# A Mamba-2 layer in fp32 halves: x's forms at other steps, the third form from a second load of x, and another order of pieces, filler and drains at two blocks of the output

## The chip, the cores and the metric

One core of one Trainium2 chip runs the whole layer. The metric is the device time of one execution in microseconds (us). TensorE (PE) multiplies, with its weight loads counted apart (PEld); VectorE (DVE) and ScalarE (ACT) work element by element; GpSimd (POOL) is used here for little but issuing the DMAs that add to what stands in SBUF; SyncE (SP) issues nearly all other DMAs, in order, and stands at one whose buffer isn't free yet.

## The reference

One layer (DEPTH is 1, so the pooling mixer isn't reached) of a Mamba-2 mixer on a sequence of 512 tokens, with an RMSNorm before it, a residual around it and a final RMSNorm. D_MODEL is 2048, D_INNER 4096, with 64 heads of 64, 8 groups, a state of 128.

```python
hn = rmsnorm(x, ln_g[0])
proj = hn @ w_in                     # 2048 -> 4096 z + 6144 (x, B, C) + 64 dt
z, xbc, dt = split(proj)
xbc = silu(causal_depthwise_conv(xbc, conv_w, conv_b))    # 4 taps
xs, B, C = split(xbc)
dt = softplus(dt + dt_bias)
a = -exp(a_log)
y = ssd_chunked_scan(xs * dt, dt * a, B, C)               # chunked state-space scan
y = (y + d_skip * xs) * silu(z)
y = rmsnorm(y, norm_g)
return rmsnorm(x + y @ w_out, final_g)
```

## The kernel before, in words

All large products are made in fp32 accuracy from halves: a tensor is split into `hi` (rounded to fp32r by a ScalarE cast, line 88) and `lo` (the rest, a VectorE subtraction, line 89), and a product is three matmuls, hi·hi, hi·lo and lo·hi. The transposed x, scaled by the norm's weight, lies in SBUF as `xh` and `xl`, 16 tiles of 128 x 512.

**Plain products.** The first eight projections, `plain`, are made directly: B0 and C0 together while x and the first weights come in, then x0, z0, x1, z1, B1 and C1, each of 16 steps (one step is the six matmuls of `mm_k`, line 211). Steps are numbered through the program: x0 begins at 32, z0 at 48, x1 at 64, z1 at 80, B1 at 96, C1 at 112, and step 128 ends them. The weights come in pieces of 8 steps (512 KB). `get_piece` loads one raw into one of the rings `ra` (3 buffers), `rb` (1) or `rc` (2) and splits it. A piece is named by its number; pieces 10 and 11 belong to z1 (steps 80 to 95), 15 to C1's second half (from step 120).

**Strassen quads.** The other 72 projections go in 36 pairs (`pair`). Each is a 2 x 2 product of blocks done with seven products instead of eight, 28 steps (`QS`) in all. For that the weights are summed into the forms T1, T2, T3 and T4 (T1 and T3 by a POOL DMA that adds in SBUF, T2 and T4 by a VectorE addition, line 618), and x into forms 1, 2, 4 (`x_forms`) and 3 (`x_form3`). `x_forms(g, j)` makes a quarter of the forms 1, 2 and 4: SP loads two halves of x once more, into `csb` and `m` (j = 0) or `h1h` and `h1l` (j = 1), ScalarE scales them, then come three VectorE combinations in an `rc` buffer (lines 576, 577, 579) and three splits (ScalarE line 573, VectorE line 574): six VectorE operations of 128 x 512 a call. `x_form3(j)` makes one of four quarters of the third form in place of the second half of `xh` and `xl`: four VectorE operations (lines 588, 589, 590, 592) through the one buffer `xr`, and a ScalarE copy. The seventh product of a quad (`last`) runs as filler between the second and the third of the next; for the first quad there is no such filler, and it begins with T1 and then R11 (`lone`).

**What runs beside it.** The dt path: 16 products, softplus on VectorE (`dt_softplus`, lines 353 to 364), cumulative sums, totals and spread (`dt_cumul`, `dt_sums`, `dt_spread`), all through the one PSUM tile `tr`; its result `sn` is stored to `cscr`, from where each unit's `csb` is loaded back for its decay (`u_load`, `u_decay`). Then for each of 32 units the convolution, transposes (line 486, into `tr`), the scan's products, the gate and a store of y.

**The output.** `blocks` gives the order: plain blocks are lists of (column quarter s, pairs of y tiles), each (s, pair) a piece of 8 steps (`mm_o`, lines 948 to 950); tuples are Strassen blocks of four `opair`s of seven products (`oproduct`, lines 886 to 888), whose forms of y are made by `y_fetch` (loads) and `y_forms`. Pieces of several pairs in one tuple of `blocks` are summed in one PSUM group, and a line of VectorE (1065) adds the group to `acc`; the accumulations of a Strassen block are lines 908, 921, 926 and so on. `load_y(p)` loads and splits the y of pair p (split on VectorE at line 758). The last plain block before a Strassen block may leave two of its four row tiles over as filler (`bridge`), which then run as `prev` between the second and third product; before, that is done at block 2 alone, and the first Strassen block runs without filler.

**What sets the order.** `add(step, f, ...)` puts an event at a step and `run(step)` issues it there. PE, SP and POOL run in the order in which the program is written; VectorE and ScalarE are ordered by the Tile scheduler, where `urgent` gives priority.

Of the kernel before, what the change touches and what calls it, by code (L numbers as in the profile page):

```python
# [18 lines left out]
P = 128  # L19
# [16 lines left out]
def mamba_layer(ctx: ExitStack, tc: tile.TileContext, d: dict, out: bass.AP):  # L36
# [99 lines left out]
    def every(*pairs):  # L136
        return [(s, pairs) for s in range(4)]

    blocks = [[(0, (0,))] + every(0, 1)[1:] + [(0, (1, 2))] + every(2)[1:], (2, 3), every(3, 12), (4, 5),
              every(13), every(14, 15)]  # L140
# [7 lines left out]
    for i, blk in enumerate(blocks):  # L148
        late = 4 if i == 0 or i > 2 and type(blocks[i - 1]) is tuple else 0
        base.append(base[-1] + (4 * QS if type(blk) is tuple else 8 * n_pieces(blk) + late))  # L150
# [404 lines left out]
    def x_forms(g, j):  # L555
# [4 lines left out]
        for n, k0 in ((n1, k), (n2, KH + k)):  # L560
            nc.sync.dma_start(n, d["xT"][:, k0:k0 + 2, :])
            for i in range(2):
                S.activation(n[:, i, :], n[:, i, :], AF.Identity, scale=lng[:, k0 + i:k0 + i + 1])
        if j == 0:
            for f, s in ((1, 0), (2, 4), (4, 8)):
                form[f, g] = [xp.tile(SSH, F32R, name=f"s{s + 2 * g + i}") for i in range(2)]
# [14 lines left out]
        put(4, t1)  # L581

    def x_form3(j):

        kk = slice(2 * j, 2 * j + 2)
        h, lo = xh[:, kk, hi_], xl[:, kk, hi_]
        t = xr[:, 3:L + 3].rearrange("p (k l) -> p k l", k=2)
        V.tensor_tensor(out=t, in0=xh[:, kk, lo_], in1=h, op=ALU.subtract)
        V.tensor_tensor(out=t, in0=t, in1=xl[:, kk, lo_], op=ALU.add)
        V.tensor_tensor(out=t, in0=t, in1=lo, op=ALU.subtract)  # L590
        S.copy(out=h, in_=t)
        V.tensor_tensor(out=lo, in0=t, in1=h, op=ALU.subtract)  # L592

# [132 lines left out]
    for g in range(1, G):  # L726
        for i in range(2):
            add(at["x", 4 * g] + 34, g_cb, g, i)
        add(at["x", 4 * g] + 34, g_bt, g)
    steps = {0: [66, 71, 63, 104, 104, 114], 1: [56, 76, 72, 108, 108, 114], NU - 1: [36, 46, 44, 65, 65, 71]}  # L730
    for u in range(5, NU - 4, UPG):
# [7 lines left out]
    for i in range(4):  # L739
        add(49 + 7 * i, x_forms, i // 2, i % 2)  # L740
        add(114 + 4 * i, x_form3, i)

# [40 lines left out]
    st = {}  # L783

    def norm_a():
        with urgent():
            st["rest"] = x_norm()
# [12 lines left out]
    add(b0 + 44, g_bt, 0)  # L800
    add(b0 + 26, dt_softplus)
    add(b0 + 37, g_cb, 0, 0)
# [179 lines left out]
    for i, blk in enumerate(blocks):  # L982
        if type(blk) is tuple:
            for s in range(4):
                q_events(len(quads) + 4 * m + s, base[i] + s * QS, s == 3, 0, 3 if s == 0 and not m else 0, s == 0 and not m)
            for j in range(2):
                add(base[i] - ((50, 32), (54, 32))[m][j], y_fetch, m, j)
                add(base[i] - ((39, 24), (47, 24))[m][j], y_forms, m, j)
            m += 1
# [39 lines left out]
    for kb, blk in enumerate(blocks[:-1]):  # L1029
# [10 lines left out]
        for s, pairs in blk:  # L1040
            ps = [None] * NC
            for p in pairs:
# [4 lines left out]
                for t in range(NC):  # L1047
                    if p == pairs[0]:
                        ps[t] = first.pop(0) if first else (ps_o or (ps_s, ps_mm)[t % 2]).tile(
                            [P, L], F32, name="mm" if ps_o or t % 2 else "S")  # L1050
                    if kb == 2 and n0 + 1 == n_end and t > 1:
                        bridge.append(partial(tail, ps[t], opieces[n0], ys[p], t, s))
                        continue
# [17 lines left out]
                n0 += 1  # L1071
                if n0 == 7:
                    ph1.close()
                    ps_o = ctx.enter_context(psum("ps_o", 6))
                    fp = ctx.enter_context(tc.tile_pool(name="fp", bufs=1))
                    load_y(2)
                    fg = fp.tile([P, DM], F32, name="fg")
                    nc.sync.dma_start(fg, d["fg"].partition_broadcast(P))
        if bridge:
            def prev(step, parts=bridge):  # L1080
                for i, f in enumerate(parts):
                    f(step + 2 * i)
                spare = ps_o.tile([P, L], F32, name="mm")
                T.transpose(spare[:, 0:P], ident, ident)

# [68 lines left out]
```

## Time and profile before

| | before |
|---|---|
| median of 3 runs | 1269.15 us (1267.62 to 1270.22) |
| the profiled execution | 1271.58 us, span 1269.6 us |
| granted TensorE clock, mean of the span | 0.992 |
| PE busy | 1235.1 us, 97% of the span |
| DVE busy | 1079.0 us, 85% |
| ACT busy | 829.0 us, 65% |
| POOL busy | 77.6 us, 6% |
| read from HBM | 211.52 MB |

The profile was taken of one execution; times in its rows are from the start of its span. A row of a timeline has its start, its duration, engine, line, operation, output and inputs, and in brackets the idle time of the engine ahead of it and what ended that. A row of waits has who waited for whom, then the total, how often and the longest. A row of windows has the stretch, its length, the busy time and the instructions of PE, PEld, DVE, ACT and POOL, then the granted clock (1 is full speed), the share of the DMA engines and GB/s. A row of DMA issues has the size of one and the median time from issue to landing.

### The profile page before, as it was taken

The numbers are of one execution on the slowest core, as the hardware profiler recorded it, in microseconds if no ns is written. First come the engines' busy times: TensorE is split into PE (matmuls) and PEld (weight loads), VectorE is DVE, ScalarE is ACT, GpSimd is POOL, SyncE is SP. The second block draws the span as 40 slices with busy tenths as digits, with TensorE's granted clock in tenths as the row PEclk, the third lists the DMA queues.
The fourth block names the chain that finished last, engine by engine and source line by source line (L and its number), as shares of the span: only waits on it lengthen the run. The fifth ranks groups of instructions, "written<-read, shape, count | busy, mean of one in ns | idle before, by whom it ended". The sixth has DMA issues, their size and how long they took to land.

```text
span 1269.6 us, 24517 instructions
## 1 busy us (share of the span) xinstructions
PE 1235.1 (97%) x9945; PEld 1178.0 (93%) x9945; DVE 1079.0 (85%) x1443; ACT 829.0 (65%) x1359; POOL 77.6 (6%) x99
## 2 busy tenths in 40 slices
PE   8989899999999999999999999999999899999997
PEld 7989899999999999999999999999888899899986
DVE  5796989998999998899989899988857887887865
ACT  7666677767767767876686777678666445444533
POOL 0000000010000000000001000000000000000000
PEclk9989999999999999999999999999999999999998
DMA  9546656767676667667676766775537576657612
GB/s 357 181 150 180 169 157 174 189 173 193 166 194 182 156 193 189 169 162 197 178 203 151 210 163 176 184 184 153 157 114 253 155 197 202 208 127 229 183 60 100
DMA packets 70193, 225.89 MB, mean 178 GB/s; under 512 B 8384, under 2 KB 12800, under 8 KB 69952
## 3 DMA queue, kind: packets, MB, share of 16 engines
q1 hardware_dynamic: 56688, 176.34, 39.5%
q0 software_dynamic: 12672, 46.14, 23.0%
q8 instruction: 78, 1.28, 0.4%
q10 hardware_dynamic: 720, 1.84, 0.4%
q14 instruction: 35, 0.29, 0.1%
HBM read 211.52 MB, written 12.78 MB: 177 GB/s over the span
## 4 chain that ended last, share of the span: by engine, by line
PE 61%; DVE 19%; ACT 8%; DMA 6%; issue 5%; SPq 0%; DVEq 0%; ACTq 0%
PE S L649 5%; PE S L651 5%; PE S L650 5%; DVE lo L89 4%; PE R L649 4%; PE R L650 3%; PE R L651 3%; PE mm L651 3%; PE mm L649 3%; PE mm L650 3%; PE mm L948 3%; PE mm L950 3%; PE mm L949 3%; PE mm L886 3%; PE mm L887 2%
## 5 line engine op out<-in xcount | busy, mean ns | idle before, releaser
L89 DVE TENSOR_TENSOR lo<-ra,hi 128x1024 fp32r<-128x1024 f32 x150 | 182.8, 1219 | 48.2 <-ACT hi L88 48.0
L88 ACT CAST hi<-ra 128x1024 fp32r<-128x1024 f32 x150 | 156.7, 1046 | 89.9 <-PE mm L887 23.5
L88 ACT CAST hi<-rc 128x1024 fp32r<-128x1024 f32 x94 | 98.9, 1053 | 99.0 <-PE mm L650 37.9
L649 PE MATMUL R<-s,hi 128*128 128x256 f32 x576 | 162.5, 282 | 0.0
L651 PE MATMUL mm<-xh,lo 128*128 128x256 f32 x576 | 159.2, 276 | 0.2 <-DVE lo L89 0.2
L649 PE MATMUL mm<-xh,hi 128*128 128x256 f32 x576 | 159.2, 276 | 0.2 <-ACT mm L705 0.2
L650 PE MATMUL R<-s,hi 128*128 128x256 f32 x576 | 159.2, 276 | 0.0
L651 PE MATMUL R<-s,lo 128*128 128x256 f32 x576 | 159.1, 276 | 0.0
L650 PE MATMUL mm<-xl,hi 128*128 128x256 f32 x576 | 159.1, 276 | 0.0
L89 DVE TENSOR_TENSOR lo<-rc,hi 128x1024 fp32r<-128x1024 f32 x94 | 114.3, 1216 | 3.9 <-ACT hi L88 3.7
L649 PEld LDWEIGHTS mm<-xh,hi 128*128 128x128 f32 x576 | 108.2, 188 | 0.6 <-ACT mm L705 0.6
L651 PEld LDWEIGHTS mm<-xh,lo 128*128 128x128 f32 x576 | 108.1, 188 | 0.4 <-DVE lo L89 0.4
L650 PEld LDWEIGHTS R<-s,hi 128*128 128x128 f32 x576 | 108.3, 188 | 0.0
L649 PEld LDWEIGHTS R<-s,hi 128*128 128x128 f32 x576 | 108.3, 188 | 0.0
L651 PEld LDWEIGHTS R<-s,lo 128*128 128x128 f32 x576 | 108.1, 188 | 0.0
L650 PEld LDWEIGHTS mm<-xl,hi 128*128 128x128 f32 x576 | 108.1, 188 | 0.0
L618 DVE TENSOR_TENSOR ra<-ra,rc 128x1024 f32<-128x1024 f32 x88 | 107.0, 1216 | 0.2
L651 PE MATMUL S<-xh,lo 128*128 128x256 f32 x288 | 79.7, 277 | 2.2 <-DVE lo L89 2.2
L649 PE MATMUL S<-xh,h1h 128*128 128x256 f32 x288 | 80.3, 279 | 1.0 <-ACT mm L705 1.0
L650 PE MATMUL S<-xl,hi 128*128 128x256 f32 x288 | 79.7, 277 | 0.7 <-DVE xl L592 0.7
L650 PE MATMUL S<-xl,h1h 128*128 128x256 f32 x288 | 80.3, 279 | 0.0
L651 PE MATMUL S<-xh,h1l 128*128 128x256 f32 x288 | 80.3, 279 | 0.0
(452 smaller groups left out, 3936.0 us busy)
## 6 DMA issues: line engine op xcount, KB each, us to landing
rc<-in_wi SPq DMA_DIRECT2D x76, 512.0 KB, 5.2
ra<-in_wi SPq DMA_DIRECT2D x42, 512.0 KB, 6.0
rb<-in_wi SPq DMA_DIRECT2D x40, 512.0 KB, 4.6
ra<-in_wi POOLq DMA_DIRECT2D x36, 512.0 KB, 6.2
rb<-in_wi POOLq DMA_DIRECT2D x36, 512.0 KB, 6.2
csb<-cscr SPq DMA_DIRECT2D x32, 512.0 KB, 5.6
ra<-in_wo SPq DMA_DIRECT2D x26, 512.0 KB, 5.2
yscr<-z SPq DMA_DIRECT2D x32, 256.0 KB, 4.4
```

The lines of the kernel that those rows point to most:

```text
L88: S.copy(out=hi, in_=raw)
L89: V.tensor_tensor(out=lo, in0=raw, in1=hi, op=ALU.subtract)
L618: V.tensor_tensor(out=raw, in0=raw, in1=qs[n][other], op=ALU.add)
L649: T.matmul(ps, hi[:, k, :], ah, start=first and k == 0, stop=False, skip_group_check=True)
L650: T.matmul(ps, hi[:, k, :], al, start=False, stop=False, skip_group_check=True)
L651: T.matmul(ps, lo[:, k, :], ah, start=False, stop=k == KH - 1, skip_group_check=True)
L886: T.matmul(ps[:, t, :], yh[:, k, tt], hi[:, k, :], start=st, stop=False, skip_group_check=True)
L887: T.matmul(ps[:, t, :], yl[:, k, tt], hi[:, k, :], start=False, stop=False, skip_group_check=True)
L948: T.matmul(ps, yh, hi, start=first and k == 0, stop=False)
L949: T.matmul(ps, yh, lo, start=False, stop=False)
L950: T.matmul(ps, yl, hi, start=False, stop=last and k == 1)
```

## The change

Three things are altered.

1. **Plain part.** `x_forms` runs at steps 38, 45, 66 and 92, in the order (1,1), (0,1), (0,0), (1,0), where it ran at 49, 56, 63 and 70 in the order (0,0), (0,1), (1,0), (1,1). Softplus is issued as urgent. The decay of unit 1 is 16 steps later.
2. **Third form.** A new `x_diff` loads a piece of x into an `ra` buffer at steps 106, 109, 122 and 124 and subtracts its second half of the tokens from its first in place. `x_form3`, now at 115, 118, 136 and 140 (before at 114, 118, 122 and 126), makes from that the high half by a scaling ScalarE activation and the low half by one VectorE operation, for each of its two tiles of 256 columns.
3. **Output.** The first plain block has another order of pieces: three pairs for s = 3 in one group, the first piece of s = 0 closed at the end. `y_fetch` and `y_forms` of the first Strassen block are 4 to 8 steps earlier with respect to its begin, the block gets the last piece's two tiles as filler and the order of the later blocks (no `lone`). The PSUM pool of the output, and `load_y(2)` with it, open after piece 6 and not 7. At both bridges a drain of TensorE stands where a spare transpose stood at the one.

```diff
-    blocks = [[(0, (0,))] + every(0, 1)[1:] + [(0, (1, 2))] + every(2)[1:], (2, 3), every(3, 12), (4, 5),
+    blocks = [[(0, (0,)), (1, (0, 1)), (2, (0, 1)), (3, (0, 1, 2)), (1, (2,)), (2, (2,)), (0, (1, 2))], (2, 3), every(3, 12), (4, 5),
...
-        late = 4 if i == 0 or i > 2 and type(blocks[i - 1]) is tuple else 0
+        late = 4 if i > 2 and type(blocks[i - 1]) is tuple else 0
...
-        if j == 0:
+        if (1, g) not in form:
...
+    diff = {}
+    def x_diff(j, name):
+        raw = load_piece(d["xT"][:, 2 * j:2 * j + 2, :], [P, 2, L], name)
+        V.tensor_tensor(out=raw[:, :, lo_], in0=raw[:, :, lo_], in1=raw[:, :, hi_], op=ALU.subtract)
+        diff[j] = raw[:, :, lo_]
     def x_form3(j):
-        kk = slice(2 * j, 2 * j + 2)
-        h, lo = xh[:, kk, hi_], xl[:, kk, hi_]
-        t = xr[:, 3:L + 3].rearrange("p (k l) -> p k l", k=2)
-        V.tensor_tensor(out=t, in0=xh[:, kk, lo_], in1=h, op=ALU.subtract)
-        V.tensor_tensor(out=t, in0=t, in1=xl[:, kk, lo_], op=ALU.add)
-        V.tensor_tensor(out=t, in0=t, in1=lo, op=ALU.subtract)
-        S.copy(out=h, in_=t)
-        V.tensor_tensor(out=lo, in0=t, in1=h, op=ALU.subtract)
+        t = diff.pop(j)
+        for i in range(2):
+            k = 2 * j + i
+            h, lo = xh[:, k, hi_], xl[:, k, hi_]
+            S.activation(h, t[:, i, :], AF.Identity, scale=lng[:, k:k + 1])
+            V.scalar_tensor_tensor(out=lo, in0=t[:, i, :], scalar=lng[:, k:k + 1], in1=h.bitcast(F32), op0=ALU.mult,
+                                   op1=ALU.subtract)
...
-    steps = {0: [66, 71, 63, 104, 104, 114], 1: [56, 76, 72, 108, 108, 114], NU - 1: [36, 46, 44, 65, 65, 71]}
+    steps = {0: [66, 71, 63, 104, 104, 114], 1: [56, 92, 72, 108, 108, 114], NU - 1: [36, 46, 44, 65, 65, 71]}
...
-        add(49 + 7 * i, x_forms, i // 2, i % 2)
-        add(114 + 4 * i, x_form3, i)
+        add((38, 45, 66, 92)[i], x_forms, *((1, 1), (0, 1), (0, 0), (1, 0))[i])
+        add((106, 109, 122, 124)[i], x_diff, i, "ra")
+        add((115, 118, 136, 140)[i], x_form3, i)
...
-    add(b0 + 26, dt_softplus)
+    add(b0 + 26, softplus)
...
-                q_events(len(quads) + 4 * m + s, base[i] + s * QS, s == 3, 0, 3 if s == 0 and not m else 0, s == 0 and not m)
+                q_events(len(quads) + 4 * m + s, base[i] + s * QS, s == 3, 0, 0, False)
             for j in range(2):
-                add(base[i] - ((50, 32), (54, 32))[m][j], y_fetch, m, j)
-                add(base[i] - ((39, 24), (47, 24))[m][j], y_forms, m, j)
+                add(base[i] - ((54, 36), (54, 32))[m][j], y_fetch, m, j)
+                add(base[i] - ((43, 28), (47, 24))[m][j], y_forms, m, j)
...
-                    if kb == 2 and n0 + 1 == n_end and t > 1:
+                    if n0 + 1 == n_end and t > 1 and kb < 4:
...
-                if n0 == 7:
+                if n0 == 6:
...
-                spare = ps_o.tile([P, L], F32, name="mm")
-                T.transpose(spare[:, 0:P], ident, ident)
+                T.drain()
```

`softplus` only wraps `dt_softplus` in `urgent`. Three places of the order show what moves.

VectorE at the low half of piece 10 (`lo<-rb`, line 89), in the order before. Lines 574 and 579 are of `x_forms` (`s_...` its forms, `rc` its buffer), line 358 is a step of softplus:

```order
L579 SCALAR_TENSOR_TENSOR rc<-rc,m 128x512
L358 SCALAR_TENSOR_TENSOR bt<-bt,z 128x256
L574 TENSOR_TENSOR s_834<-rc,s_833 128x512
L358 SCALAR_TENSOR_TENSOR bt<-bt,z 128x256
L574 TENSOR_TENSOR s_836<-rc,s_835 128x512
L358 SCALAR_TENSOR_TENSOR bt<-bt,z 128x256
L89 TENSOR_TENSOR lo<-rb,hi 128x1024
```

The same place in the order after; line 404 is a tap of x0's convolution:

```order
L404 SCALAR_TENSOR_TENSOR xs<-xr,par,xs 128x512
L358 SCALAR_TENSOR_TENSOR bt<-bt,z 128x256
L404 SCALAR_TENSOR_TENSOR xs<-xr,par,xs 128x512
L358 SCALAR_TENSOR_TENSOR bt<-bt,z 128x256
L89 TENSOR_TENSOR lo<-rb,hi 128x1024
L358 SCALAR_TENSOR_TENSOR bt<-bt,z 128x256
L576 TENSOR_TENSOR rc<-m,csb 128x512
```

The third call of `x_forms` now begins behind the low half, where before it ended ahead of it. The fourth has moved on to the end of the dt path; VectorE there, in the order after, down to the copy of `sn` (line 389) and one row more:

```order
L378 TENSOR_TENSOR nwl<-tr,cs 128x256
L576 TENSOR_TENSOR rc<-m,csb 128x512
L379 TENSOR_TENSOR win<-nwl,tr 128x64
L577 SCALAR_TENSOR_TENSOR rc<-rc,csb 128x512
L574 TENSOR_TENSOR s_508<-rc,s_507 128x512
L489 TENSOR_TENSOR xd<-tr,dt 128x512
L579 SCALAR_TENSOR_TENSOR rc<-rc,m 128x512
L574 TENSOR_TENSOR s_510<-rc,s_509 128x512
L389 COPY sn<-tr 64x512
L574 TENSOR_TENSOR s_512<-rc,s_511 128x512
```

All but the last of its six operations stand ahead of that copy. SP around the new loads of x (`ra<-in_xT`), as the order after has it from the load of `csb` for unit 0 on:

```order
L453 DMA csb<-cscr 128x1024
L456 DMA ecs<-escr 64x256 x2
L82 DMA rc<-in_wi 128x1024
L82 DMA ra<-in_xT 128x1024
L82 DMA rc<-in_wi 128x1024
L82 DMA ra<-in_xT 128x1024
L82 DMA ra<-in_wi 128x1024
L453 DMA csb<-cscr 128x1024
L456 DMA ecs<-escr 64x256 x2
L82 DMA rc<-in_wi 128x1024
L82 DMA rb<-in_wi 128x1024
L82 DMA ra<-in_xT 128x1024 x2
```

The last two of the four loads stand one behind the other, ahead of the next `rc` load of the first quad, the store of unit 0's y and the third quad's first load. At the entry of the output's first Strassen block, VectorE's order before was (908: the accumulation of the block's first T1; `f4l`, `f3l`, `f22l`: forms; 618: the sum T2; 921 and 926: the accumulations of the third and the fourth product):

```order
L908 TENSOR_TENSOR acc<-acc,mm 128x2x256
L860 TENSOR_TENSOR f4l<-yt,f4h 128x512
L860 TENSOR_TENSOR f3l<-yr,f3h 128x512
L860 TENSOR_TENSOR f22l<-yr,f22h 128x512
L618 TENSOR_TENSOR ra<-ra,rc 128x1024
L971 SCALAR_TENSOR_TENSOR acc<-xt,rms,acc 128x512
L89 TENSOR_TENSOR h1l<-ra,h1h 128x1024
L89 TENSOR_TENSOR lo<-ra,hi 128x1024
L89 TENSOR_TENSOR lo<-rc,hi 128x1024
L89 TENSOR_TENSOR lo<-rb,hi 128x1024
L618 TENSOR_TENSOR ra<-ra,rc 128x1024
L921 TENSOR_TENSOR acc<-acc,mm 128x2x256
```

After, with the lines 920, 938 and 933 for 908, 926 and 921, 625 for 618, 872 for 860 and 1039 for the filler's accumulations:

```order
L872 TENSOR_TENSOR f22l<-yr,f22h 128x512
L625 TENSOR_TENSOR ra<-ra,rc 128x1024
...
L625 TENSOR_TENSOR ra<-ra,rc 128x1024
L89 TENSOR_TENSOR h1l<-ra,h1h 128x1024
L920 TENSOR_TENSOR acc<-acc,mm 128x2x256
L89 TENSOR_TENSOR lo<-rc,hi 128x1024
L1039 TENSOR_TENSOR acc<-mm,acc 128x512 x2
L938 TENSOR_TENSOR acc<-acc,mm 128x2x256
L89 TENSOR_TENSOR lo<-rb,hi 128x1024
L933 TENSOR_TENSOR acc<-acc,mm 128x2x256
```

The forms and the first sum now stand ahead of the block's first accumulation, and the two tiles of filler between that and the fourth product's.

## What was predicted, before the changed kernel had run

> **What bounds the kernel now.** I read the page first, then TensorE's waits, then the stretches around the longest of them.
>
> ```profile
> span 1269.6 us, 24517 instructions
> ...
> PE 1235.1 (97%) x9945; PEld 1178.0 (93%) x9945; DVE 1079.0 (85%) x1443; ACT 829.0 (65%) x1359; POOL 77.6 (6%) x99
> ```
>
> TensorE is busy for all but 34.5 us. The change takes no product away, so it can win only waits, and what the clock loses behind them. The waits of PE, with total, count and longest:
>
> ```profile
> PE yo L211 <- ACT xh L194: 6.1, 1, 6.1
> PE S L211 <- DVE lo L89: 3.9, 1, 3.9
> PE tr L486 <- ACT xs L407: 3.1, 8, 1.4
> PE mm L886 <- DVE acc L926: 2.3, 1, 2.3
> PE S L651 <- DVE lo L89: 2.2, 1, 2.2
> PE mm L888 <- DVE lo L89: 1.4, 1, 1.4
> ...
> PE tr L386 <- DVE xd L489: 1.0, 1, 1.0
> PE S L649 <- ACT mm L705: 1.0, 1, 1.0
> PE mm L886 <- ACT hi L88: 0.9, 1, 0.9
> PE S L650 <- DVE xl L592: 0.7, 1, 0.7
> PE tr L486 <- DVE win L379: 0.6, 1, 0.6
> ```
>
> The 6.1 is the start, which isn't touched. The others named by a single event lie in three places, as the timeline of PE shows (a wait stands in brackets):
>
> ```profile
> 79.88 0.63 PE L211 MATMUL S<-xh,hi 128*128 128x256 f32 x2
> ...
> 81.16 0.63 PE L211 MATMUL S<-xh,hi 128*128 128x256 f32 x2
> ...
> 97.39 0.40 PE L211 MATMUL mm<-xh,hi 128*128 128x256 f32 x2
> ...
> 98.10 0.40 PE L211 MATMUL mm<-xh,hi 128*128 128x256 f32 x2
> ...
> 138.31 0.39 PE L651 MATMUL S<-xh,lo 128*128 128x256 f32 x1 [2.16 <-DVE lo L89]
> ...
> 1006.15 0.36 PE L886 MATMUL mm<-hi,f3h 128*128 128x256 f32 x1 [2.26 <-DVE acc L926]
> ```
>
> Place A is 75 to 97 us (3.9, 0.6, 1.0), in the plain pieces. Place B is 136 to 160 us (2.2, 0.7, 1.0, 1.4), the first Strassen quad. Place C is 995 to 1007 us (0.9, 1.4, 2.3), the entry of the output's first Strassen block. Behind each the clock is halved; stretches with the busy time of PE, PEld, DVE, ACT, POOL, then the granted clock:
>
> ```profile
> 44.00:98.00 54.00, 48.41 (x353) 46.34 (x353) 50.51 (x85) 33.06 (x49) 1.00 (x1) 0.94 0.43 147
> ...
> 79.30:85.30 6.00, 6.00 (x28) 6.00 (x29) 6.00 (x13) 4.15 (x6) 0.00 (x0) 0.50 0.95 343
> 143.40:146.80 3.40, 3.40 (x18) 3.40 (x17) 3.36 (x5) 1.05 (x1) 0.00 (x0) 0.50 1.01 404
> 1007.00:1010.40 3.40, 3.40 (x18) 3.40 (x18) 2.62 (x4) 0.00 (x0) 0.88 (x1) 0.50 0.44 105
> ```
>
> A step of the plain products (six matmuls) takes 98.10 - 97.39 = 0.71 us at full clock and 81.16 - 79.88 = 1.28 at half, so a half-clock stretch loses 45%: 2.7 in A, 1.5 in B, 1.5 in C. All that stands to be won is A 5.5 + 2.7 = 8.2, B 5.3 + 1.5 = 6.8, C 4.6 + 1.5 = 6.1, together 21.1 us.
>
> **Part by part.**
>
> *A: x's forms at steps 38, 45, 66, 92, softplus urgent.* The wait of 3.9 is for the low half of weight piece 10, which stood behind three form groups on VectorE:
>
> ```profile
> 75.21 0.68 DVE L579 SCALAR_TENSOR_TENSOR rc<-rc,m 128x512 f32<-128x512 f32 x1
> 75.81 0.41 DVE L358 SCALAR_TENSOR_TENSOR bt<-bt,z 128x256 f32<-128x256 f32 x1
> ...
> 78.02 1.22 DVE L89 TENSOR_TENSOR lo<-rb,hi 128x1024 fp32r<-128x1024 f32 x1
> ...
> 96.88 0.68 DVE L389 COPY sn<-tr 64x512 f32<-64x512 f32 x1
> ```
>
> In the new order only two groups stand ahead of it. One group is six operations; the next start comes 75.81 - 75.21 = 0.60 later, so 3.6 us go, and with them two softplus steps (0.41 each, 0.7 in all, since these overlap too): it starts at about 78.0 - 4.3 = 73.7. PE gets it at 78.02 + 1.22 = 79.2 now and waits 3.9, so it wants it at 75.3: in time, with 0.4 to spare. The 3.9 and its clock go. But the work isn't gone: VectorE is busy 50.51 of 54.0 us from 44 to 98, and all four groups still stand ahead of the copy of sn at 96.88, but for one operation. What can move that copy is the idle 3.5, that operation (0.6) and the gate that now stands behind it (0.6), less about 0.7 that the second use of h1h and h1l waits for its load: 4.0 us earlier, about 92.9. PE's step 96 needs it, so PE is there 4.0 earlier and not 8.2. The rest comes back as new waits: for piece 11's low half (about 1), and for the one PSUM tile tr, which softplus' sums, xs's transposes and the spread of cs take in turn, each released by VectorE behind whole weight splits (about 3). What follows hangs on the same copy:
>
> ```profile
> 97.59 0.51 SPq L390 DMA_DIRECT2D cscr<-sn  x1
> ...
> 103.02 0.34 SPq L453 DMA_DIRECT2D csb<-cscr  x1
> ```
>
> ```profile
> 106.65 0.40 ACT L469 ACTIVATE m<-csb,cs 128x128 f32<-128x128 f32 x1 [5.11 <-DMA csb<-cscr]
> ```
>
> The store of cs, its load back, ScalarE's decay, the mask product and piece 15's low half follow it, which PE wants at step 120. This chain moves by the same 4.0, less about 0.2 since ScalarE writes half of m later, ahead of which SP won't load csb. I take A as 3.8. Below, the tr waits of up to 2.5 at one place may halve the clock again (1.5, in part absorbed, since PE would wait at step 120 anyway) and each guess on VectorE may be off by a microsecond: 1.5. Above: 8.2.
>
> [...]
>
> *B: third form from x loaded once more, decay of unit 1 later.* The old form:
>
> ```profile
> L590 DVE TENSOR_TENSOR xr<-xr,xl 128x512 f32<-128x512 f32 x4 | 2.8, 690 | 0.1
> ```
>
> Each of four calls has four such operations: 16 x 0.69 = 11.0 us. Now it has one, and two of 256 columns, which I put at 0.42, between half of 0.69 and all of it: 4 x (0.69 + 0.84) = 6.1. VectorE is rid of 4.9 us, and nothing of it waits for xr any more. T3's low half, late by 2.16, moves up by that, by A's 3.8, and by ScalarE doing its high half within the decay and not after it; it is there some 3 us ahead of PE. C1's normalisation leaves its bank early, so the next quad's S takes a bank that is free (1.0 goes), and xs of unit 2 is done as PE comes (1.4 goes). What is added is four loads of x on SP, into the ring of three ra buffers. The fourth finds all three held: SP stands at it until the third is used, and a load of the first quad's weights, a store of y and the third quad's first load wait behind it. The third's two operations stand behind this one in the new order:
>
> ```profile
> 130.46 0.41 DVE L492 TENSOR_TENSOR xw<-xd,win 128x256 f32<-128x256 f32 x1
> ```
>
> With them, 0.84, and A's 3.8 ahead that is 130.9 + 0.8 - 3.8 = 127.9. The trace has x's halves loaded in two ways:
>
> ```profile
> m<-in_xT SPq DMA_DIRECT2D x2, 512.0 KB, 3.7
> ...
> h1l<-in_xT SPq DMA_DIRECT2D x2, 512.0 KB, 6.0
> ```
>
> so it lands at 131.6 to 133.9. Difference (0.69), cast (put at the same) and two low halves (0.84) take 2.2 more: 133.8 to 136.1. PE came to T3 at 138.31 - 2.16 = 136.15, so now at 132.3, and this load holds the last of the four quarters of x: T3 is 24 matmuls, 4 steps of 0.71, and three quarters of it are 2.1, so it is wanted at 134.4. A wait of 0 to 1.7; I take 0.4, near the fast end, since few loads are on their way there. B: 6.8 - 0.4 = 6.4, from 3 to 6.8.
>
> *C: order of the pieces, filler, drains.* In before, the block starts with an empty filler, and its forms come late: T2's add is behind five forms' low halves, and the accumulator that T3's bank waits for is behind a split whose weights were still on their way:
>
> ```profile
> 1004.18 1.23 DVE L89 TENSOR_TENSOR lo<-ra,hi 128x1024 fp32r<-128x1024 f32 x1 [2.04 <-ACT hi L88]
> 1005.32 0.68 DVE L926 TENSOR_TENSOR acc<-acc,mm 128x512 f32<-128x512 f32 x1
> ```
>
> Now the forms are eight steps earlier, in time in which VectorE waited for PE, four accumulations fewer stand there (three pairs in one PSUM group), and two tiles of the last piece fill PE between second and third product. In the new order L926's successor stands behind splits whose data have landed. All 6.1 go. Two prices: y of pair 2 is wanted one piece earlier, and its load is issued one piece earlier, but not much earlier than VectorE allowed:
>
> ```profile
> 962.07 1.41 DVE L758 SCALAR_TENSOR_TENSOR ybl<-ra,par,ybh 128x512 fp32r<-128x512 f32 x2
> ```
>
> It was done at 963.5. A piece is 8 steps of 0.71, 5.7 us: if load and operation move by as much, it is done at 957.8, and since it now also stands ahead of the second forms on VectorE nothing keeps it: 0 (up to 3, if it keeps half of its time). And the drains: no row shows one between matmuls; the nearest is
>
> ```profile
> 1120.34 0.40 PE L950 MATMUL mm<-oh,ybl 128*128 128x512 f32 x1
> ```
>
> whose 0.40 it may expose whole, or not at all: 0.2 each, 0.4 for two. C: 5.7, from 1 to 6.1.
>
> *Sum.* 3.8 + 6.4 + 5.7 = 15.9 us. The profiled execution took 1271.58 us (span 1269.6 and 2.0 around it): 1255.7. The median of the runs shown, 1269.15, is 2.4 below it, so 1253.3.
>
> **Rivals.** (1) *VectorE keeps more of A and B.* For: it is busy 50.51 of 54. If tr's waits halve the clock and the fourth load lands late, A gives 1.5 and B 4.0: 11.2 in all, 1258.0. (2) *C is only moved.* If y of pair 2 is 3 us late and clock goes with it, C gives 1.2: 1257.8. Against: its load and order move along. (3) *All goes.* If VectorE packs better than I count: 21.1, 1248.1. Against: the sum of its work. (4) *Slower: the ra ring stays late.* The loads behind the fourth x load start late:
>
> ```profile
> ra<-in_wi SPq DMA_DIRECT2D x42, 512.0 KB, 6.0
> ...
> ra<-in_wi POOLq DMA_DIRECT2D x36, 512.0 KB, 6.2
> ```
>
> A quad's first weights need 6.0 to land, a split, and 6.2 for the sum on top: some 15 us of lead. For the third quad SP comes to that load some 5 us behind the fourth x, at 133, and PE to its place 88 steps of 0.71 behind step 96 at 92.9, at 155: 22. Below 15, every one of 34 further quads would wait, unless the ring catches up; at 0.6 each 20.4 are lost: 1273.7. It decides from 15.9 / 34 = 0.47 a quad. Against: a ring slot is free 17 steps ahead of the next load's place, so a late ring recovers. (5) *The change doesn't do what it says:* the orders of VectorE and ScalarE are a scheduler's, and the waits come back elsewhere in full: 1269.
>
> **Chances.** Forecast 0.50, (1) 0.18, (2) 0.12, (3) 0.14, (4) 0.03, (5) 0.03. The range goes from just under (3) to over (1) and (2), with a little for the clock: 1247.5 to 1261.0; 0.2% of this kernel, 2.5 us, is about what its measurement can tell. Faster 0.94, same 0.03, slower 0.03.
>
> **What would show it.** Right: no wait for lo L89 near 75; step 96 at 92 to 94; tr waits of 2 to 3 us between 85 and 92; T3 of the first quad without a wait of 2; PE without a gap from the output's first piece to its second block; no half clock at 143 or 1007. Wrong: a gap at the y of pair 2; SP late at R11 of every quad; the clock halved around 88; step 96 at 90 or less (then VectorE had room that I don't see).

## The result, and the profile after

The changed kernel takes 1259.0 us (median of 4 runs, 1257.6 to 1260.8) against 1268.4 of before, measured beside it: ratio 0.9926, 95% interval 0.9910 to 0.9941, so 9.4 us are won where 15.9 were forecast. The two profiled executions, 1271.58 and 1259.74, lie 11.8 apart. The time is inside the range; the sum was 6.5 us too large.

The page of the changed kernel and its waits of PE:

```profile
span 1258.0 us, 24522 instructions
...
PE 1230.7 (98%) x9944; PEld 1174.2 (93%) x9944; DVE 1071.5 (85%) x1435; ACT 829.0 (66%) x1363; POOL 77.7 (6%) x99
```

```profile
PE yo L211 <- ACT xh L194: 6.0, 1, 6.0
PE S L211 <- DVE lo L89: 3.6, 1, 3.6
PE tr L486 <- DVE win L379: 2.1, 1, 2.1
PE yd L446 <- ACT bc L407: 1.8, 1, 1.8
PE mm L961 <- DVE lo L89: 1.4, 1, 1.4
PE mm L960 <- DVE z L663: 1.1, 1, 1.1
PE tr L486 <- ACT xs L407: 1.0, 6, 0.2
```

The four waits of the first quad (place B) and the three of the output's first Strassen block (place C) are gone. The row `S L211 <- lo L89` looks as in before, 3.6 for 3.9, but it is another wait: that of step 81 is gone, and this one is at step 120, for piece 15. Two more are new, 1.8 at step 69 and 1.4 at the begin of the fifth block, and the one for `tr` behind `win` has grown from 0.6 to 2.1. The granted clock at two places that were halved before, and at the two that are halved now; the granted clock is the third number from the end:

```profile
91.10:94.40 3.30, 3.30 (x17) 3.17 (x17) 3.06 (x6) 2.39 (x4) 0.00 (x0) 0.50 0.91 119
115.00:118.30 3.30, 3.21 (x15) 3.22 (x16) 3.30 (x8) 1.84 (x3) 0.00 (x0) 0.50 0.25 56
143.40:146.80 3.40, 3.40 (x32) 3.40 (x32) 3.40 (x5) 1.95 (x4) 0.00 (x0) 1.00 1.01 411
1007.00:1010.40 3.40, 3.40 (x31) 3.40 (x31) 2.48 (x3) 1.06 (x1) 0.00 (x0) 1.00 1.04 363
```

At 143 and 1007 the clock is whole now, as it is near 79; behind the wait for `tr` (91) and behind the new one at step 120 (115) it is halved. What stood behind VectorE's part of the new wait, in the timeline of DVE:

```profile
106.59 2.33 DVE L404 SCALAR_TENSOR_TENSOR bc<-xr,par,bc 128x512 f32<-128x512 f32 x3
111.53 0.69 DVE L588 TENSOR_TENSOR ra<-ra 128x512 f32<-128x512 f32 x1 [2.62 <-DMA ra<-in_xT]
112.14 1.75 DVE L474 TENSOR_TENSOR m<-m,cbm 128x1536 f32<-128x1536 f32 x1
113.81 1.22 DVE L89 TENSOR_TENSOR lo<-rc,hi 128x1024 fp32r<-128x1024 f32 x1
```

And ScalarE's, which gives the mask product (line 474) its input and the low half its high half:

```profile
105.13 0.40 ACT L469 ACTIVATE m<-csb,cs 128x128 f32<-128x128 f32 x1 [4.74 <-DMA csb<-cscr]
...
108.67 1.05 ACT L472 ACTIVATE m<-m 128x1024 f32<-128x1024 f32 x1
109.62 1.03 ACT L88 CAST hi<-rc 128x1024 fp32r<-128x1024 f32 x1
```

Both inputs were there by 110.7. VectorE stood 2.62 us at line 588, the subtraction of the first extra load of x, until the load had landed, with the mask product and piece 15's low half behind it in its order. The mask product began at 112.14; by its inputs it could have begun at 109.7, 2.4 earlier.

Differences between the two traces at the same matmul (before less after, from their timelines of PE): step 96 is reached 2.8 us earlier (96.60 and 93.79), step 120 2.9 (113.64 and 110.70), step 126 2.4 us later (117.96 and 120.35), unit 2's transposes 5.4 earlier (159.20 and 153.83), the output's product that waits for `z` 7.3 (919.08 and 911.82), the same matmul of the sixth product of the output's first Strassen block 13.6 (1010.10 and 996.46), the last matmul's end 11.4 (1261.06 and 1249.66).

### The profile page after: what moved, and what is told of

Read it like the earlier page. It is cut to its first block, busy times and chain, and to the rows that moved or that the text cites. A ratio compares the mean times of both kernels' runs of the same rounds, so it can differ in the third digit from the quotient of the medians.

```text
span 1258.0 us, 24522 instructions
## 1 busy us (share of the span) xinstructions
PE 1230.7 (98%) x9944; PEld 1174.2 (93%) x9944; DVE 1071.5 (85%) x1435; ACT 829.0 (66%) x1363; POOL 77.7 (6%) x99
## 3 DMA queue, kind: packets, MB, share of 16 engines
q8 instruction: 78, 1.28, 0.4%
## 4 chain that ended last, share of the span: by engine, by line
PE 65%; DVE 17%; ACT 8%; DMA 5%; issue 5%; SPq 0%; DVEq 0%; ACTq 0%
PE S L658 5%; PE S L656 5%; PE S L657 5%; PE R L656 4%; PE R L657 4%; PE R L658 4%; PE mm L898 4%; PE mm L899 3%; PE mm L900 3%; DVE lo L89 3%; PE mm L658 3%; PE mm L656 3%; PE mm L657 3%; PE mm L960 3%; PE mm L962 3%
## 5 line engine op out<-in xcount | busy, mean ns | idle before, releaser
L89 DVE TENSOR_TENSOR lo<-ra,hi 128x1024 fp32r<-128x1024 f32 x150 | 182.9, 1219 | 47.5 <-ACT hi L88 47.1
L89 DVE TENSOR_TENSOR lo<-rc,hi 128x1024 fp32r<-128x1024 f32 x94 | 114.3, 1217 | 4.0 <-ACT hi L88 4.0
L658 PE MATMUL S<-s,lo 128*128 128x256 f32 x288 | 79.5, 276 | 0.0
L656 PE MATMUL S<-xh,hi 128*128 128x256 f32 x288 | 79.5, 276 | 0.0
```

The source lines that it names most:

```text
L89: V.tensor_tensor(out=lo, in0=raw, in1=hi, op=ALU.subtract)
L656: T.matmul(ps, hi[:, k, :], ah, start=first and k == 0, stop=False, skip_group_check=True)
L658: T.matmul(ps, lo[:, k, :], ah, start=False, stop=k == KH - 1, skip_group_check=True)
```

## The experiments

The times are medians, the ratios are to before on the same chip, with their 95% intervals; runs of one kernel spread over 3 to 9 us, so differences of 1 to 2 us between medians mean little without their intervals. A trace shows one execution. In four of the kernels below it was the shortest of all, 3.6 to 6.1 us under the median (the first two parts together, everything but the third form, and the two with the loads of x earliest), so their waits say where time goes and not how much a median execution loses.

**The three parts alone, and two together.** The later decay of unit 1 goes with the third form here. Before with x's forms and urgent softplus alone:

```
+ add((38, 45, 66, 92)[i], x_forms, *((1, 1), (0, 1), (0, 0), (1, 0))[i])
+ add(b0 + 26, softplus)          # third form, decay and output as before
```

> The kernel before with one part of the change alone: x's forms at steps 38, 45, 66, 92 and softplus urgent; old third form, old decay step, old output. Theory: no load of x stands ahead of piece 15's low half, so the wait at step 120 is 1.5 or less; the wait of 1.8 at step 69 is there, the 3.9 at step 81 is gone, so TensorE is about 2 us ahead at step 121, the waits of the first quad stay near 5.3, and the time is 2 to 3 us less than before: 1266. Rival (the cs chain is late by itself): the wait at step 120 is over 3 here too, the clock is halved behind it, and the time is 1269 to 1271, not faster than before.

1267.8 us, ratio 0.9989 (0.9976 to 1.0002): not told apart from before. Its waits of PE:

```profile
PE tr L486 <- ACT xs L407: 4.3, 8, 2.0
...
PE S L651 <- DVE lo L89: 2.0, 2, 1.6
PE yd L446 <- ACT bc L407: 2.0, 1, 2.0
PE S L211 <- DVE lo L89: 1.7, 2, 1.4
```

Step 120 costs 1.4 here, without an extra load of x, and the 2.0 at step 69 is there: both as the theory has it, though the time is less than its 2 to 3 us below before. The decay of unit 0 begins at 105.17, and TensorE comes to step 120 at 111.5; in the changed kernel these are 105.13 and 111.4. So of the 3.64 there, 1.35 are left without the load, and 2.3 are the load's.

Before with the third form and the decay alone:

```
+ x_diff at 106, 109, 122, 124; x_form3 at 115, 118, 136, 140; steps[1]: 76 -> 92
```

> The kernel before with the third form from the extra load of x and the later decay alone. Theory: here the subtraction stands behind piece 15's low half in VectorE's order, so the load costs nothing at step 120; all four waits of the first quad and its halved clock go, 6.8 us: about 1261.6. Rival (the place needs the head start that the earlier forms were to give): T3's low half is still 1 to 2 us late and the clock is halved again, 3 to 4 us are won: 1265.

1271.1 us, ratio 1.0021 (1.0011 to 1.0032): slower than before. Neither the theory nor its rival had that.

```profile
PE S L211 <- DVE lo L89: 4.4, 2, 4.1
PE S L656 <- ACT sn L702: 2.9, 1, 2.9
PE S L657 <- DVE xl L598: 1.6, 1, 1.6
PE S L656 <- ACT xh L597: 1.5, 1, 1.5
```

The old four waits of the quad are gone and three others stand there, 5.9 us in all: for the copy of S that T3 needs (line 702), and for the last quarter of the third form, whose load comes late (lines 597 and 598). The clock is halved twice there, from 137.0 and from 143.8, where in before it was halved once. ScalarE's part:

```profile
132.68 1.05 ACT L88 CAST hi<-rb 128x1024 fp32r<-128x1024 f32 x1 [1.60 <-DMA rb<-in_wi]
...
135.98 0.35 ACT L702 COPY sn<-S 128x256 f32<-128x256 f32 x1
```

It stood for the sum T3 in `rb`, in the midst of unit 1's decay, and the copy came after both.

The output alone:

```
+ blocks, late, q_events, y_fetch, y_forms, bridge, n0 == 6, T.drain(): as changed; all else as before
```

> The kernel before with the output's part alone: order of the pieces, earlier forms of y, filler, drains. Theory: the three waits of 995 to 1007 and the halved clock go (6.1), the new wait for a low half of weights at the begin of the fifth block comes (1.4, there was 0.0): 4.7 less, 1263.7. Rival (the drains cost what a matmul's end takes, and slow TensorE behind them): matmuls of the first Strassen block are spaced 0.118 and not 0.113 us, 2 us more: 1265.7.

1263.1 us, ratio 0.9947 (0.9934 to 0.9960): 5.6 by the medians, 6.7 by the ratio. The theory's 4.7 was a little low, and the rival's 1265.7 is out, though the block's matmuls have the slower spacing that it named (0.118 us); no half clock (the span's mean is 0.996, against 0.992 in before) and no wait over 0.5 is left at the first Strassen block, and the new one stands at the fifth block:

```profile
PE mm L953 <- DVE lo L89: 1.5, 1, 1.5
```

The first two parts together, old output:

```
+ x_forms, softplus, x_diff, x_form3, steps[1] as changed; output as before
```

> The kernel before with the plain part and the third form of the change, and the old output. Theory (the first two parts only pay together, the output's part stands by itself): alone they gave 0.9 and -2.4, together 9.6 - 5.6 = 4.0, so 1264.5 to 1265.5; the waits of 1.3 and 2.3 to 2.5 at the output's first Strassen block are there and the first quad has none over 0.5, with one of 3 to 4 at step 120. Rival (the sum of the parts alone, and the output's part is worth more beside them): 1270.

1266.1 us, ratio 0.9976 (0.9966 to 0.9987): 3.0 by the ratio, nearer to the theory's 4.0 than to the rival. With the output's 6.7 that makes 9.7, against 9.4 for the whole: the output's part stands by itself. The first two give 1.4 and -2.7 alone (by the ratios) and 3.0 together. Their trace has 2.6 at step 120, a little under the 3 to 4 expected, and no wait over 0.4 in the first quad.

Everything but the third form:

```
- x_diff; x_form3 and its steps as before; all else as changed
```

> The changed kernel with the old third form at its old steps, no extra load of x; x's forms, softplus, the later decay and the output as changed. Theory (the third form pays only beside the earlier forms): x's forms and softplus alone gave 0.9 (1267.8 against 1268.7), the output alone 5.6, the new third form alone cost 2.4, and the three together gave 9.4 to 9.8; so without the third form 6 to 7 are won, 1262.0 to 1263.0, and the new third form is worth 3 to 4 beside the others. The wait at step 120 is 1.5 or less, that of the first quad for T3's low half 1.6, for unit 2's transposes about 2. Rival (the new third form costs here what it costs alone, and the rest is more than the sum): 1256 to 1257.

1265.3 us, ratio 0.9980 (0.9963 to 0.9997), so the new third form is worth 6.9 us (by the ratios) beside the other parts, more than the 3 to 4 expected, where alone it cost 2.7. The trace, of the shortest of twelve executions (1261.45), shows only some of that. Its longest wait is for unit 2's input:

```profile
PE tr L486 <- ACT xs L407: 8.0, 12, 6.1
```

C1's normalisation (line 411, through `xr`) runs at 134.95 here. In the changed kernel it runs at 121.91, as soon as its product ends, since nothing holds `xr`:

```profile
134.95 0.69 DVE L411 TENSOR_TENSOR xr<-S,rbc 128x512 f32<-128x512 f32 x1
```

```profile
121.91 0.69 DVE L411 TENSOR_TENSOR xr<-S,rbc 128x512 f32<-128x512 f32 x1 [1.29 <-PE S L211]
```

But VectorE ends unit 2's input at the same time in both. The last operation here, with ScalarE's silu behind it, and the same operation in the changed kernel:

```profile
152.23 0.75 DVE L404 SCALAR_TENSOR_TENSOR xs<-xr,par,xs 128x512 f32<-128x512 f32 x1
154.86 0.63 ACT L407 ACTIVATE xs<-xs 128x512 f32<-128x512 f32 x1
```

```profile
152.26 0.74 DVE L404 SCALAR_TENSOR_TENSOR xs<-xr,par,xs 128x512 f32<-128x512 f32 x1
```

So most of the 6.1 is TensorE coming early: it is there at 149.4, and at 153.8 in the changed kernel, which had stood 3.6 at step 120 where this one stood 1.1. The rest is ScalarE, whose silu is 1.8 later than the 153.04 of the changed kernel, with a part of the next decay (lines 469 to 471) and two table loads of 1.28 ahead of it. The clock is halved from 153.4 to 160.4. What the third form gives is seen where TensorE comes early with it: unit 2's last operation ends at 150.9 with the first two parts together and at 150.0 in the next run, not 153.0, and TensorE does not wait.

**The load that VectorE stands for.** The changed kernel with the first two extra loads ahead of the store of cs:

```
- add((106, 109, 122, 124)[i], x_diff, i, "ra")
+ add((94, 95, 122, 124)[i], x_diff, i, "ra")
```

> The changed kernel, with the first two extra loads of x at steps 94 and 95, ahead of the store of cs on SP, and not at 106 and 109. Theory (VectorE stands for a load): in the changed kernel VectorE stood 2.62 us for the first extra load of x, and the mask product and piece 15's low half stood behind it; now the load lands before 101, the subtraction falls into VectorE's idle 7.65 us, TensorE's wait at step 120 goes from 3.64 to about 1.1 (mask product from 109.7, 1.75, low half 1.2, against 111.4), and the 3.4 us of halved clock behind it (1.7) go: 4.2 less than the changed kernel, profiled about 1255.5, ratio to before about 0.989. Rival (the chain of cs is late by itself, through its store, its load back and ScalarE's decay): the wait stays above 3 and the time at 1259.

1257.9 us, ratio 0.9915 (0.9898 to 0.9932): not told apart from the changed kernel. In its trace the wait at step 120 is 0.3, and the clock isn't halved there (0.998 in the mean of the span), so the rival's wait of over 3 is out. But the load alone does not make that difference. ScalarE's order changed too: it writes the second part of `m` (line 394) ahead of the gate's silu here and behind it in the changed kernel, the load of csb follows that on SP, and the decay begins at 101.39 and not at 105.13. The load's own 2.3 is shown by the run with x's forms alone. What was won is taken back in the first quad:

```profile
PE S L656 <- ACT sn L702: 1.0, 1, 1.0
PE S L656 <- ACT xh L597: 0.9, 1, 0.9
PE S L657 <- DVE xl L598: 0.6, 1, 0.6
```

```profile
134.95 0.69 DVE L588 TENSOR_TENSOR ra<-ra 128x512 f32<-128x512 f32 x1 [1.45 <-DMA ra<-in_xT]
```

The fourth load, which SP issued at 129.8, is awaited there. In the changed kernel it lands at 137.9 and nobody waits, because TensorE comes later: the stop at step 120 had hidden it.

The changed kernel with none of the loads in a full ring:

```
+ add((94, 95, 98, 116)[i], x_diff, i, ("ra", "ra", "rb", "ra")[i])
+ add((115, 118, 120, 126)[i], x_form3, i)
```

> The changed kernel with all four extra loads of x at other steps, so that none finds its ring full: two into ra at 94 and 95, the third into rb at 98, the fourth into ra at 116; the third form at 115, 118, 120 and 126. Theory (the wait moved): the changed kernel's first quad had no waits only because TensorE came 5.3 us later to it; with the first two loads moved, 2.5 us came back there, 1.5 of it for the last quarter of the third form, whose load was issued at 129.8. Now it is issued near 111, so those 1.5 go, the wait for the copy of S (1.0) may stay, and the time is 1.5 to 2.5 less than with the first two loads moved alone: profiled about 1255.5, median about 1256. Rival (VectorE's sum of work sets the first quad, whatever is loaded when): the waits come back under other names and the median stays at 1258 or above.

1258.3 us, ratio 0.9914 (0.9901 to 0.9927). The two waits for the last quarter are gone, but the one for the copy of S has grown to 2.7. Timeline of ScalarE:

```profile
123.86 1.06 ACT L88 CAST hi<-rc 128x1024 fp32r<-128x1024 f32 x1 [5.36 <-DMA rc<-in_wi]
...
131.97 1.05 ACT L88 CAST hi<-rb 128x1024 fp32r<-128x1024 f32 x1 [1.94 <-DMA rb<-in_wi]
...
135.93 0.35 ACT L702 COPY sn<-S 128x256 f32<-128x256 f32 x1
```

So the theory holds for the load, and the rival for the time.

All loads ahead of step 106, and x's second forms at 57:

```
+ add((94, 95, 98, 100)[i], x_diff, i, ("ra", "ra", "rb", "ra")[i])    # second difference kept in the first's buffer
+ add((115, 118, 120, 122)[i], x_form3, i)
+ add((38, 57, 66, 92)[i], x_forms, ...)
```

> The changed kernel with all four extra loads of x ahead of step 106: two into ra at 94 and 95, the third into rb at 98, the fourth into ra at 100 (the second difference is kept in the free half of the first one's buffer, so that a buffer comes free); the third form at 115, 118, 120, 122; the second call of x's forms at 57. Theory (crowded loads): with the fourth load at 112 the first quad's rc and rb loads took 7 and 14 us to land, ScalarE stood 5.4 and 1.9 for them, and the copy of S behind that held TensorE for 2.7. With no load of x from 106 on that wait falls to 1 or less, the one at step 69 is gone, step 120 stays below 0.5: 1254 to 1255. Rival (ScalarE's order holds the copy of S, with unit 1's decay ahead of it, whenever the loads land): a wait of 2 to 3 stays there and the median is 1257 to 1258.

1257.8 us, ratio 0.9922 (0.9901 to 0.9943). The first quad has no wait over 0.3, as expected of the early loads, and the one at step 69 is gone; but 3.2 us came back at step 120 (0.6 and 2.6), against the expectation, by the same mechanism: VectorE stood for the third load.

```profile
105.45 0.69 DVE L589 TENSOR_TENSOR rb<-rb 128x512 f32<-128x512 f32 x1 [8.23 <-DMA rb<-in_xT]
```

The last one is as the one before it, x's second forms at 57 included, with these loads in another order:

```
+ add((94, 95, 98, 105)[i], x_diff, ...); third and fourth subtraction moved into x_form3
+ add((115, 118, 119, 121)[i], x_form3, i)
```

> As the run with all loads of x early and the second call of x's forms at 57, but the fourth load stands behind that of piece 15, and the third and fourth difference are taken where the third form is made (steps 119 and 121). Theory (VectorE and ScalarE stand for loads in their order): there, the two loads of x kept piece 15's weights until 107.8, VectorE stood for the third load until 105.5 ahead of the convolution and for the fourth, and TensorE waited 3.2 at step 120 with 1.7 of halved clock; with the order of loads changed that wait falls to 1 or less and the first quad stays free of waits over 1: profiled about 1251, median 1254 to 1255. Rival (the waits go round: what is won at one place is lost at the next, since VectorE has the same work to do by step 152): waits of 2 to 3 in the first quad, median 1257 to 1258.

Its profiled execution is the shortest of all, 1253.79, with 0.8 at step 120 and 1.7 in the first quad:

```profile
PE S L665 <- ACT sn L711: 1.7, 1, 1.7
...
PE S L211 <- DVE lo L89: 0.8, 1, 0.8
```

But its six runs go from 1253.8 to 1262.7, the median is 1259.9, and the ratio 0.9922 (0.9900 to 0.9944) is that of the changed kernel. One trace with fewer waits is not yet a faster kernel. No version here is shown to beat the changed one.

**Softplus, and the second call of the forms.** The changed kernel with that call later:

```
- add((38, 45, 66, 92)[i], x_forms, ...)
+ add((38, 57, 66, 92)[i], x_forms, ...)
```

> The changed kernel with the second call of x's forms at step 57 and not 45, so that its load doesn't hold VectorE ahead of C0's convolution. Theory: TensorE's 1.83 at step 69 goes, the wait of 3.9 at step 81 doesn't come back; but step 120 hangs on the first extra load of x and on the store of cs, not on TensorE, so most of the 1.8 is given back there (its wait grows to about 5) and the median is 0 to 0.7 below the changed kernel's 1259.0. Rival (the chain behind it moves along): all 1.8 are won, 1257.2.

1258.7 us, ratio 0.9907 (0.9893 to 0.9922). The wait at step 69 is gone and step 81 stays free, as expected; step 120's is 2.8, not 5, since the copy of sn came earlier too. The interval overlaps that of the changed kernel, so what was won can't be told.

The changed kernel without softplus as urgent:

```
- add(b0 + 26, softplus)
+ add(b0 + 26, dt_softplus)
```

> The changed kernel without softplus as urgent. Theory: C0's silu no longer stands behind softplus' exponential and its table load on ScalarE, and TensorE's 1.83 at step 69 falls to 0.5 or less; softplus ends later on VectorE, so the waits for tr between steps 88 and 96 grow by 1 to 3, the store of cs and the wait at step 120 move with it: 1258 to 1261. Rival (softplus as urgent is what took the 3.9 at step 81 away): that wait comes back by 2 us or more and the median is over 1262.

1268.8 us, ratio 0.9992 (0.9981 to 1.0003): the whole gain is gone. The theory misses. The rival has the time, over 1262, but not the wait: step 81's didn't come back. Step 69's fell to 0.7, near the theory's 0.5, but:

```profile
PE tr L370 <- DVE bt L364: 3.6, 1, 3.6
PE S L211 <- DVE lo L89: 3.3, 1, 3.3
PE S L656 <- ACT xh L597: 2.6, 1, 2.6
PE S L657 <- DVE xl L598: 1.7, 1, 1.7
```

```profile
85.87 0.43 DVE L364 SCALAR_TENSOR_TENSOR bt<-dt,dab 128x256 f32<-128x256 f32 x1
```

The last step of softplus (line 364) ends at 86.3; TensorE stood 3.6 for it. In the changed kernel it runs here:

```profile
81.49 0.41 DVE L364 SCALAR_TENSOR_TENSOR bt<-dt,dab 128x256 f32<-128x256 f32 x1
```

Without the priority the wait at step 81 is only moved by ten steps.

**The drains.** The changed kernel with a spare transpose at both bridges:

```
- T.drain()
+ spare = ps_o.tile([P, L], F32, name="mm"); T.transpose(spare[:, 0:P], ident, ident)
```

> The changed kernel with the spare transpose of before in place of the drain at both bridges. Theory (a drain costs 0.2 each or less): no difference, 1258.5 to 1259.2, and the spacing of matmuls in the first Strassen block of the output is 0.118 us, as in the changed kernel. Rival (the drain puts TensorE in step with its weight loads at the slower spacing): 0.113 to 0.114 through that block, 2 us less: 1257.

1261.1 us, ratio 0.9940 (0.9926 to 0.9954), some 2 us above the theory's time, but its interval overlaps that of the drains. The spacing of the matmuls is the slower one here too (0.118 us), so the rival is out; whether a drain is cheaper than a spare transpose stays open, since this trace has a wait of 2.1 at 895 us, far from the bridges.

## Why the prediction was right or wrong, point by point

- **A, the low half of piece 10.** Right: no wait at step 81, no half clock at 78. Forecast for step 96 were 92 to 94 and a wait for `tr` of 2 to 3 between 85 and 92: 93.8 and 2.1. The copy of sn came 2.7 us earlier (94.17, not 96.88) where 4.0 were forecast, so the head start at step 120 was 2.9 and not 3.8. The price of softplus was misjudged: it went into the sum as two steps of 0.7, and without its priority the whole gain is gone. One of the prediction's signs of being wrong came as well: the clock is halved behind the wait for `tr`, from 91.0 to 94.5. What that costs is already in the 93.8 at step 96.
- **A, "this chain moves by the same 4.0".** This is the step that failed, at two links. The first is ScalarE: of the 2.7 that the copy of sn came earlier, the decay kept 1.5 (105.13, not 106.65), so 1.2 were lost where 0.2 were put. The second part of `m` (line 394), whose store SP issues ahead of the load of csb, stayed behind the gate's silu and came only 1.2 earlier (99.98, not 101.15). The second link is VectorE. The working followed the chain to piece 15's low half, but the extra loads of x only on SP. It did not look at who stands behind the first user of such a load on VectorE: the subtraction, put ahead of the mask product by the scheduler, stood 2.62 us for its data, and the mask product came 2.4 later than its inputs allowed. So the low half was done 0.9 later than in before (115.03, not 114.15), and TensorE came 2.8 earlier to the matmul that needs it: 3.64 at step 120, and 1.7 of clock behind it. A gave -2.4 at step 126 instead of 3.8. Without the load the wait is 1.4 (x's forms alone); with the load moved and the decay begun 3.7 earlier it is 0.3. The 1.8 at step 69 is of a like kind: VectorE stood 3.2 us for the second call's x, which ScalarE could scale only when it had landed, ahead of C0's convolution, and ScalarE then had softplus' exponential ahead of C0's silu.
- **B.** All 6.8 went, 6.4 were forecast. The difference at unit 2's transposes against that at step 126 is 7.8, of which 6.8 are the waits and the halved clock; no run separates the rest. But the reason was half right. The freed `xr` counts (C1's normalisation 20.7 us earlier than 142.58 in before): with the third form alone the two waits that hang on it, 1.0 and 1.4, went, and those for T3's data came back in other places. The fourth load, priced at 0 to 1.7, was issued at 133.7 and not at 127.9, landed 4.2 later, and was free only because TensorE came late; with an early TensorE it costs 1.5, and the copy of S, which the working did not have, 0.7 to 2.9 in five runs.
- **C.** All of the waits and the halved clock went, 6.1; forecast 5.7. The y of pair 2 made no wait. Alone it gave 5.6 to 6.7. Not seen was the wait at the fifth block, 1.4: its first weights' cast stands on ScalarE behind one for a load of the last pieces, and TensorE comes there earlier relative to that load.
- **The sum** of the traces: -2.4 at step 126, then 7.8 for B, 1.9 up to the output (0.8 of it small waits of before that aren't there now; no run separates the rest), 6.4 around C, -2.2 after it. That is 11.4, up to rounding, at the last matmul's end.
- **The rivals.** The time fell near to the first rival's 1258.0, but by another mechanism: B did not keep anything. Half of its condition held: the clock was halved behind the wait of 2.12 for `tr` at 88.8 (0.50 from 91.1 to 94.4), as behind the 3.64 at step 120 (0.50 from 115.0 to 118.3).

What stays open: why the first two parts together give 4.3 us more than the sum of the two alone is shown only in its waits, not settled by a run of its own; that everything but the third form gives less than the output alone (0.9980 against 0.9947) goes with the 6.1 at unit 2's transposes and the clock behind it, but these are of an execution 3.8 us under the median, so what the median loses isn't shown. Moving the load took the wait at step 120 away and not the time, so the 3.64 is explained, but no run shows its price in the median. Why runs of one kernel differ by 3 to 9 us isn't shown by any trace here.

## What to carry to other kernels

When a load is added, look on each engine for its first user and for what is queued behind that: the scheduler here put it ahead of work whose data were there sooner, and VectorE, keeping its order, then stood for the DMA, 2.62 us in the changed kernel and 8.23 with all loads early, with other engines' work behind it. A wait that is removed uncovers the next: four versions took the wait at step 120 or those of the first quad away and none was told apart from the changed kernel. Parts of a change to one chain don't add up (1.4 and -2.7 alone, 3.0 together), while a part at another place does (6.7).

## What the runs showed of the hardware

Matmuls of 256 columns ran at two paces in these traces with the granted clock at 1.00. In the output's first Strassen block, before, after, and with the first two loads moved (38 us each, PE's instructions in brackets):

```profile
1012.00:1050.00 38.00, 38.00 (x338) 38.00 (x337) 31.11 (x33) 16.11 (x19) 3.43 (x4) 1.00 0.72 197
```

```profile
999.00:1037.00 38.00, 38.00 (x325) 38.00 (x325) 31.20 (x35) 16.76 (x19) 3.43 (x4) 1.00 0.70 192
```

```profile
990.00:1028.00 38.00, 38.00 (x337) 38.00 (x337) 31.85 (x35) 16.70 (x18) 3.43 (x4) 1.00 0.71 183
```

From start to start within a product that is 0.1135 and 0.1178 us a matmul, the slower one in the changed kernel. The changed kernel kept the slower one through the whole block, which took back 2.0 us of C's gain (the difference falls from 13.6 to 11.6 at the block's last matmul); the same instructions with other loads 900 us earlier ran at the faster one (337 in 38 us, against 325). What sets it isn't known.

In these traces the length of a wait did not decide alone whether the clock was halved. In the run without a load in a full ring TensorE stood still for 2.7 and the clock stayed whole (1.00 from 136.4 to 140.0); in the last run of x's loads a wait of 1.5, with one of 0.45 behind it, was followed by a halved clock (0.50 from 88.4 to 91.5). The run before that one had the same two waits, 1.51 and 0.45, and its clock was 1.00 from 88.8 to 92.2. Single waits of 2.12 and 2.13 differ in the same way: behind the first, in the changed kernel, the clock was halved (91.0 to 94.5), and in the run with a spare transpose, where 0.49 followed the 2.13, it was not (the mean clock of the span was 0.997 there and 0.995 in the changed kernel).

```profile
133.60:136.30 2.70, 0.00 (x0) 0.00 (x0) 2.38 (x5) 2.70 (x9) 0.00 (x0) 1.00 0.03 6
136.40:140.00 3.60, 3.60 (x32) 3.60 (x33) 3.60 (x4) 2.30 (x3) 0.00 (x0) 1.00 0.95 182
```

```profile
85.10:88.40 3.30, 1.36 (x11) 1.16 (x10) 3.30 (x8) 1.25 (x2) 1.00 (x1) 0.97 0.83 281
88.40:91.50 3.10, 3.08 (x15) 2.97 (x16) 2.54 (x5) 1.73 (x3) 0.00 (x0) 0.50 0.92 162
```
